# Two-level block matmul on one core: a new order of the steps in a group, and five sums on GpSimd in place of six

## The chip, the cores and the metric

One core of one Trainium2 chip runs the kernel. The metric is the device time of one execution in microseconds; of the kernel before there are three timed runs and one profiled execution. The engines are called as in the profile: PE is TensorE (matmul), PEld its weight load, DVE is VectorE, ACT is ScalarE, POOL is GpSimd, SP is SyncE, whose queue issues the DMAs.

## The reference

```python
def setup_inputs():
    B, S, D = 8, 2048, 2048
    return {
        "x": np.random.randn(B, S, D).astype(np.float32),
        "w": np.random.randn(D, D).astype(np.float32),
    }

def reference(x, w):
    cs = np.cumsum(x, axis=1)
    diff = cs - np.concatenate([np.zeros((cs.shape[0], 1, cs.shape[2]), dtype=np.float32), cs[:, :-1, :]], axis=1)
    return np.matmul(diff, w).astype(np.float32)
```

The differences of a running sum are the numbers themselves, so the output is x times w: 16384 rows by 2048, with 2048 in the contraction.

## The kernel before

The 16384 rows are 128 tiles of 128 rows. Four tiles are multiplied plainly at the start, while w comes in; then tiles are taken in groups of four. From row tile 12 on there are 29 groups, and each runs the same list of named steps (class Group, L988). The four tiles of a group are called g, h, k and l. The weights stay in SBUF as fp16 blocks, and each x tile is scaled row by row into fp16, so that the product can be made from block sums with fewer multiplications (Strassen's scheme in Winograd's form), on two levels.

The outer level makes the sums S1 to S4 of x blocks (128x1024, DVE, L1188 to L1193) and seven products P1 to P7 of a group. Six of these (all but P6) are split once more in the same way. The names of the inner steps, for a product Pn:

- Pn.s1 to Pn.s4: four sums of x quarters, 128x512 fp16, both inputs in SBUF, one instruction each. `total` (L559) puts it on DVE (L563) or, if its name stands in ON_POOL (L557), on POOL (L561).
- Pn.fp4 and the like: a fill, one DVE instruction (128x2048 fp16, L958) that makes a difference of two weight blocks in the tile `flow`, which the quarter Pn.p4 then reads. Both its inputs are in SBUF too. There are eight fills in a group.
- Pn.p1 to Pn.p7: the quarters, four matmuls each (L592). P6 takes eight such pieces (L573).
- merges (m1, a5g, a7k and so on, L1062), copies (cg, c5, cv) and snapshots from one PSUM bank to another or to a tile c: DVE and ACT.
- keep.C.. (ACT), add.C.. (DVE, L603 and L1128), last.C.. (ACT, L600): they bring a piece of the result out of PSUM into a tile c. A DVE step of these reads one input from PSUM. put.C.. (SP) stores it.
- load, weigh0, weigh1, scale, recip, unit, narrow0, narrow1, turn0, turn1 of g, h, k, l: they bring in the x tile of a later group, find a row's size on ACT (L125), turn it into a factor on POOL (scale, unit: L142, L161) and DVE (recip: L156), narrow it to fp16 on ACT (L172) and transpose it by DMA (turn, L185).

A program-wide list, ORDER (L1271), holds all 215 steps of a group in the order in which they are issued. "+1" behind a name means that the step is run for the group after the current one, "+2" for the one after that, "-1" for the one before. `after` (L86) keeps each engine's instructions in that order, so ORDER sets six in-order queues, one for each engine and one for the DMAs. Between engines only data sets the time: an instruction waits for the semaphores of what it reads and of the last readers of the buffer it writes, and then runs as soon as its own queue is free. Small sums live in four scratch quarters (`scratch`, L984): a sum takes the quarter that an earlier product's step has let go, and so waits for that step.

Tiles as the profile names them: x is a transposed x tile, `inner` holds the scratch quarters and some weights, b is a PSUM bank, c a result piece, `flow` the fill, F the loaded x, `of` a row's numbers.

Of the kernel before, what the change touches and what calls it, by code (L numbers as in the profile page):

```python
# [10 lines left out]
def kernel(  # L11
# [540 lines left out]
    def less(dst, p, q):  # L552
        if len(dst.shape) == 4 or len(p.shape) == 4 or len(q.shape) == 4:
            dst, p, q = in_twos(dst), in_twos(p), in_twos(q)
        after("dve", lambda: nc.vector.tensor_tensor(dst, p, q, SUB))

    ON_POOL = "P3.s1 P3.s4 P4.s1 P4.s3 P4.s4 P5.s4".split()  # L557

    def total(dst, p, q, op, pool=False):  # L559
        if pool:  # L560
            after("pool", lambda: nc.gpsimd.tensor_tensor(dst.all, p.all, q.all, op))  # L561
        else:
            after("dve", lambda: nc.vector.tensor_tensor(dst.all, p.all, q.all, op))  # L563
# [479 lines left out]

# [227 lines left out]
    ORDER = """  # L1271
    S1.h+0 S2.h+0 last.C12h1-1 put.C21h1-1 put.C12h1-1 last.C11g1+0 S4.h+0 keep.C22g0+0
    P3.p2+0 P6h.3+0 P5.s1+0 keep.C12g0+0 weigh0.g+1 add.C12g0.z+0 P6h.0+0 P6h.2+0
    P6h.1+0 weigh1.g+1 add.C11h0.q+0 S3.g+0 P5.s3+0 keep.C12g1+0 P7.p1+0 P4.p1+0
    put.C11g1+0 P7.fp5+0 P3.s1+0 put.C11h0+0 S3.h+0 scale.g+1 recip.g+1 P7.s1+0 P7.c1+0
    P3.s3+0 P7.s2+0 put.C11h1+0 P7.a1+0 narrow0.g+1 P7.s3+0 P7.p5+0 P7.s4+0 P7.p6+0
    P7.p2+0 P7.fp7+0 keep.C12h1+0 P5.s2+0 P7.c5+0 P5.p5+0 keep.C21g0+0 P7.c6+0
    add.C22g0.x+0 P7.a5g+0 narrow1.g+1 P4.s1+0 P7.a5h+0 P5.s4+0 P5.ct+0 P7.a6+0 load.h+1
    P7.p7+0 P4.p2+0 add.C21g0.x+0 P4.s2+0 P5.p6+0 turn0.g+1 put.C21g0+0 P7.c7+0 P7.p3+0
    P3.s2+0 weigh0.h+1 P3.p1+0 P5.m1+0 P5.p3+0 weigh1.h+1 P7.a7h+0 put.C22g0+0  # L1280
    add.C12g0.q+0 P5.fp4+0 P5.p7+0 last.C12g0+0 P3.s4+0 turn1.g+1 P3.p6+0 P4.p6+0
    keep.C22g1+0 P5.m2+0 P5.p4+0 scale.h+1 unit.l+0 add.C22g1.x+0 recip.h+1
    add.C12g1.q+0 keep.C12h0+0 P3.p7+0 P3.p3+0 P7.a7k+0 narrow0.h+1 keep.C22h0+0
    put.C12g0+0 keep.C22h1+0 narrow1.h+1 P7.fp4+0 add.C12h1.q+0 add.C12h0.q+0
    add.C12h1.z+0 add.C22h1.x+0 P4.s3+0 unit.g+1 P7.p4+0 keep.C21h1+0 P3.p4+0 P4.p5+0
    P4.s4+0 add.C12h0.z+0 P3.p5+0 put.C22g1+0 keep.C21g1+0 P4.fp4+0 add.C12g1.z+0
    add.C22h0.x+0 add.C12g1.e+0 load.k+1 P4.p3+0 last.C12h0+0 weigh0.k+1 turn0.h+1
    P2.p1+1 P1.p1+1 weigh1.k+1 last.C12g1+0 turn1.h+1 P1.cg+1 add.C21g1.x+0 P1.s1+1
    scale.k+1 recip.k+1 put.C22h0+0 narrow0.k+1 put.C22h1+0 P4.p4+0 P1.s2+1 P1.p5+1
    add.C21g1.q+0 P1.s4+1 P2.s1+1 add.C21h1.e+0 P1.ct+1 put.C12h0+0 P2.s2+1 narrow1.k+1  # L1290
    P1.p6+1 put.C12g1+0 keep.C11g0+1 P1.m1+1 P4.p7+0 add.C21h1.q+0 P1.p2+1 P1.s3+1
    P1.p3+1 load.l+1 P1.p7+1 unit.h+1 unit.k+1 P1.fp4+1 last.C21g1+0 keep.C21h0+0
    P2.s4+1 turn0.k+1 add.C21h0.x+0 P1.m2+1 keep.C11g1+1 P2.p6+1 add.C11g1.q+1 P2.cv+1
    weigh0.l+1 keep.C11h1+1 P2.s3+1 P2.p2+1 P2.p5+1 weigh1.l+1 P1.p4+1 add.C11g0.v+1
    add.C11h1.e+1 turn1.k+1 last.C21h1+0 P2.p7+1 scale.l+1 put.C21h0+0 recip.l+1
    add.C12h1.e+0 S1.g+1 P2.p3+1 P5.p1+1 narrow0.l+1 S2.g+1 P2.fp4+1 P6g.0+1 P6g.1+1
    add.C11h1.q+1 narrow1.l+1 P2.p4+1 add.C11g1.e+1 P5.cg+1 P5.p2+1 put.C21g1+0
    put.C11g0+1 S4.g+1 P3.fp2+1 turn0.l+1 keep.C11h0+1 turn1.l+1 load.g+2 last.C11h1+1
    P6g.3+1 P6g.2+1
    """  # L1300
# [81 lines left out]
```

## Time and profile before

| what | before |
|---|---|
| three timed runs | 1456.04, 1457.63, 1458.39 us (median 1457.63) |
| the profiled execution | 1461.91 us, of which its instructions span 1459.8 us |
| mean granted clock of PE | 0.999 |
| busy: PE, DVE | 1428.9 us (98%), 1398.8 us (96%) |
| busy: ACT, POOL | 1159.6 us (79%), 356.7 us (24%) |
| large sums on POOL (L561) | 174, six in each of 29 groups |
| moved by DMA | 351.65 MB, mean 241 GB/s |

A row of the timeline gives the start in microseconds from the span's start, the duration, engine, line, operation, tiles and shape, and in brackets the idle time before it with what ended it. Rows of one engine whose starts lie closer together than their durations are pipelined: the next instruction starts before the last one's end is recorded. What an instruction costs its engine is then the distance between starts, not the duration. The windows view gives the busy time of each engine in a stretch, with the number of its instructions in brackets. The table of waits gives, for each engine and line, what ended its idle time: the sum in microseconds, how often, and the longest.

### The profile page before, as it was taken

To read this page: it belongs to the slowest core of one execution; us is meant where nothing else is said; L and a number is where in the kernel's file an instruction comes from. 1 tells how busy PE (TensorE), PEld (TensorE's weight loads), DVE (VectorE), ACT (ScalarE), POOL (GpSimd) and SP (SyncE) were. 2 spreads that over 40 slices of the span, in tenths; PEclk is the share of its full clock that TensorE was granted. 3 is DMA by queue.
4 is the path that set the end of the run, shared out by engine and by line. 5 is a ranking of instruction groups with operands and counts; after the bars stand their busy time and mean duration, and the time that the engine had idled before them with its cause. 6 is when DMAs were issued, how large, how long until landed. Compare 5 with 4: busy or idle time off the path is not lost. (4 is left out here: it accounts for less than half of the span.)

```text
span 1459.8 us, 21125 instructions
## 1 busy us (share of the span) xinstructions
PE 1428.9 (98%) x6567; PEld 634.9 (43%) x6567; DVE 1398.8 (96%) x2354; ACT 1159.6 (79%) x1782; POOL 356.7 (24%) x422
## 2 busy tenths in 40 slices
PE   8999999999999999999999999999999999999997
PEld 3444444444444444444444444444444444444443
DVE  7998879999999999999999999999999999999998
ACT  5887568888878888888888888888888888878882
POOL 0101022122322122322223332223321223321221
PEclk9999999999999999999999999999999999999999
DMA  9999858989889999998998899998889988889982
GB/s 361 364 238 299 214 159 224 251 230 237 243 234 232 260 222 245 237 244 228 257 233 246 233 239 237 251 220 251 239 240 238 245 229 257 235 238 238 246 236 104
DMA packets 377761, 351.65 MB, mean 241 GB/s; under 512 B 274800, under 2 KB 274800, under 8 KB 377520
## 3 DMA queue, kind: packets, MB, share of 16 engines
q1 hardware_dynamic: 377088, 348.47, 87.9%
q0 software_dynamic: 560, 1.84, 0.4%
q8 instruction: 51, 0.84, 0.2%
q14 instruction: 62, 0.51, 0.1%
HBM read 150.99 MB, written 134.22 MB: 195 GB/s over the span
## 5 line engine op out<-in xcount | busy, mean ns | idle before, releaser
L592 PE MATMUL b<-W,x 128*128 128x512 f16 x2116 | 519.5, 379 | 5.7 <-DVE x L563 4.1
L592 PEld LDWEIGHTS <-x 128*128 128x128 f16 x2936 | 284.7, 98 | 366.9 <-DVE x L563 17.0
L1128 DVE TENSOR_TENSOR c<-b,c 128x512 f32<-128x512 f32 x504 | 333.5, 680 | 1.8 <-PE b L592 1.7
L172 ACT ACTIVATE F<-F,of 128x1024 f16<-128x1024 f32 x246 | 282.9, 1150 | 32.0 <-DVE of L156 30.4
L125 ACT ACTIVATE waste<-F 128x1024 uint8<-128x1024 f32 x246 | 259.9, 1057 | 56.9 <-DMA F<-in_x_dram 53.8
L592 PEld LDWEIGHTS <-inner 128*128 128x128 f16 x1984 | 190.7, 98 | 248.9 <-DVE inner L563 26.9
L592 PE MATMUL b<-W,inner 128*128 128x512 f16 x1168 | 286.5, 379 | 3.7 <-DVE b L1062 2.3
L573 PE MATMUL b<-W,x 128*128 128x512 f16 x1248 | 285.4, 379 | 1.5 <-DVE x L563 1.3
L603 DVE SCALAR_TENSOR_TENSOR c<-b,of,c 128x512 f32<-128x512 f32 x286 | 210.3, 743 | 12.8 <-PE b L592 5.8
L563 DVE TENSOR_TENSOR x<-x,x 128x1024 f16<-128x1024 f16 (+1 forms) x358 | 211.7, 598 | 10.2 <-DMA x<-F 6.7
L592 PE MATMUL b<-flow,x 128*128 128x512 f16 x812 | 208.3, 379 | 4.8 <-DVE flow L958 3.7
L600 ACT ACTIVATE c<-b,of 128x512 f32<-128x512 f32 x268 | 178.4, 682 | 38.1 <-PE b L592 13.7
L142 POOL TENSOR_SCALAR of<-of 128x1 f32<-128x1 f32 x112 | 80.7, 721 | 474.2 <-ACT waste L125 409.4
L1062 DVE TENSOR_TENSOR b<-b,c 128x512 f32<-128x512 f32 x284 | 188.4, 691 | 1.9 <-ACT c L1087 1.0
L1117 ACT COPY c<-b 128x512 f32<-128x512 f32 x224 | 128.6, 580 | 74.1 <-DVE c L603 46.1
L573 PEld LDWEIGHTS <-x 128*128 128x128 f16 x1248 | 121.6, 98 | 150.0 <-DVE x L563 9.2
L958 DVE TENSOR_TENSOR flow<-W 128x2048 f16<-128x2048 f16 x142 | 179.0, 1260 | 0.0
L600 ACT ACTIVATE c<-c,of 128x512 f32<-128x512 f32 x224 | 154.8, 714 | 14.0 <-DVE c L1128 13.9
L592 PE MATMUL b<-inner 128*128 128x512 f16 x472 | 121.1, 379 | 0.0
L561 POOL TENSOR_TENSOR inner<-x 128x512 f16<-128x512 f16 x29 | 35.8, 1234 | 269.0 <-PE b L592 259.1
L561 POOL TENSOR_TENSOR x<-x,x 128x512 f16<-128x512 f16 x58 | 89.7, 1547 | 21.4 <-PE b L592 21.4
L1087 ACT COPY c<-b 128x512 f32<-128x512 f32 x112 | 66.0, 589 | 24.5 <-PE b L592 10.6
(78 smaller groups left out, 983.9 us busy)
## 6 DMA issues: line engine op xcount, KB each, us to landing
F<-in_x_dram SPq DMA_DIRECT2D x246, 512.0 KB, 5.9
out_dram<-c SPq DMA_DIRECT2D x492, 256.0 KB, 3.2
W<-in_w_dram SPq DMA_DIRECT2D x32, 512.0 KB, 10.1
...
```

The costliest lines, as they stand in the source:

```text
L125: lambda: nc.scalar.activation(waste, where[t][i], ABS, scale=1.0 / ROW, accum_out=sums_of[t][:, i : i + 1],),
L172: lambda: nc.scalar.activation(narrowed(t)[:, ds(i * NH, NH)], where[t][i], COPY, scale=s),
L561: after("pool", lambda: nc.gpsimd.tensor_tensor(dst.all, p.all, q.all, op))
L563: after("dve", lambda: nc.vector.tensor_tensor(dst.all, p.all, q.all, op))
L573: said = nc.tensor.matmul(to[n], a[k], b[k][:, n, :], start=(first and k == 0), stop=(k == KH - 1), skip_group_check=True,)
L592: said = nc.tensor.matmul(to, a[k], b[k], start=(first and k == 0), stop=(k == 3), skip_group_check=True)
L600: after("act", lambda: nc.scalar.activation(c, p, COPY, scale=u))
L603: after("dve", lambda: nc.vector.scalar_tensor_tensor(c, p, u, c, MUL, ADD))
L958: after("dve", lambda: nc.vector.tensor_tensor(in_twos(flow), x, y, op))
L1062: after("dve", lambda: nc.vector.tensor_tensor(t, p, s, ADD))
L1117: after("act", lambda: nc.scalar.copy(to, p))
L1128: after("dve", lambda: nc.vector.tensor_tensor(to, p, to, ADD))
```

## The change

ON_POOL names five sums where there were six: P1.s4, P2.s3, P4.s2, P4.s4 and P5.s4. P3.s1, P3.s4, P4.s1 and P4.s3 go from POOL to DVE, and P1.s4, P2.s3 and P4.s2 from DVE to POOL. ORDER is a new list of the same 215 steps, and its round begins at another point (so some steps that stood as "+0" at its front now stand as "+1" at its end, and weigh0.g, weigh1.g and scale.g as "+2"). Two smaller tables follow from it: in which slots the first group's plain P7 is run (PLAINLY), and which step the first group's one-off weight difference stands before (add.C12h1.e in place of add.C12g1.e). No instruction's shape changes, and the arithmetic is the same.

Cut to its core, with one piece of the list before and after:

```diff
-    ON_POOL = "P3.s1 P3.s4 P4.s1 P4.s3 P4.s4 P5.s4".split()
+    ON_POOL = "P1.s4 P2.s3 P4.s2 P4.s4 P5.s4".split()
...
-    P1.p6+1 put.C12g1+0 keep.C11g0+1 P1.m1+1 P4.p7+0 add.C21h1.q+0 P1.p2+1 P1.s3+1
-    P1.p3+1 load.l+1 P1.p7+1 unit.h+1 unit.k+1 P1.fp4+1 last.C21g1+0 keep.C21h0+0
+    add.C21h1.e+0 P1.ct+1 P1.s4+1 P1.p6+1 unit.k+1 P1.m1+1 P4.p4+0 P4.p7+0 narrow1.k+1
+    add.C21g1.x+0 P2.s1+1 keep.C11g0+1 last.C12h1+0 add.C21h1.q+0 P2.s2+1 P2.cv+1
+    P1.fp4+1 P1.p3+1 keep.C11g1+1 keep.C21h0+0 P1.p7+1 P2.s4+1 weigh0.l+1 turn1.k+1
...
-        "P7.p5": ["P7g.1"],
+        "P7.p5": ["P7g.0", "P7g.1"],
...
-"add.C12g1.e": lambda: less(in_7.t12, in_7.t12, in_7.t11)
+"add.C12h1.e": lambda: less(in_7.t12, in_7.t12, in_7.t11)
```

What stands on POOL in a group, before (two places apart, from the same round of the list). Each row is line, operation, output and inputs, shape; x_63 to x_70 are the eight halves of the four transposed x tiles (x_63 and x_64 of g, x_65 and x_66 of h, x_67 and x_68 of k, x_69 and x_70 of l). The two long runs of sums here are P4.s1, P5.s4, P3.s4, and then P4.s3 and P4.s4; P3.s1 comes last:

```order
L561 TENSOR_TENSOR x_67<-x_70 128x512
L561 TENSOR_TENSOR inner<-x_67,inner 128x512
L561 TENSOR_TENSOR inner<-x_64,inner 128x512
L142 TENSOR_SCALAR of<-of 128x1
L161 TENSOR_SCALAR of<-of,uw 128x1
L561 TENSOR_TENSOR x_70<-x_68,x_70 128x512
L161 TENSOR_SCALAR of<-of,uw 128x1
L561 TENSOR_TENSOR x_69<-x_68,x_67 128x512
L142 TENSOR_SCALAR of<-of 128x1
L161 TENSOR_SCALAR of<-of,uw 128x1 x2
L142 TENSOR_SCALAR of<-of 128x1
L561 TENSOR_TENSOR inner<-x_66 128x512
```

And after, from P1.s4 (the first sum) over P2.s3 and P5.s4 to P4.s2 and P4.s4:

```order
L561 TENSOR_TENSOR inner<-x_63,inner 128x512
L161 TENSOR_SCALAR of<-of,uw 128x1
L561 TENSOR_TENSOR inner<-x_64,x_66 128x512
L142 TENSOR_SCALAR of<-of 128x1 x2
L161 TENSOR_SCALAR of<-of,uw 128x1
L561 TENSOR_TENSOR inner<-x_67,inner 128x512
L142 TENSOR_SCALAR of<-of 128x1
L161 TENSOR_SCALAR of<-of,uw 128x1
L561 TENSOR_TENSOR x_67<-x_67,x_68 128x512
L561 TENSOR_TENSOR x_69<-x_68,x_67 128x512
```

Of the sums only P5.s4 and P4.s4 are on POOL in both; the small instructions between them (scale and unit) are the same in number.

On DVE, around the fill P1.fp4 (the row that reads S_775), before:

```order
L1062 TENSOR_TENSOR b_788<-b_785,c_763 128x512
L1128 TENSOR_TENSOR c_755<-b_787,c_755 128x512
L563 TENSOR_TENSOR inner<-x_63,x_65 128x512
L958 TENSOR_TENSOR flow<-W,S_775 128x2048
L563 TENSOR_TENSOR inner<-x_64,inner 128x512
L603 SCALAR_TENSOR_TENSOR c_751<-b_789,of,c_751 128x512
L1062 TENSOR_TENSOR b_791<-b_785,c_763 128x512
L1128 TENSOR_TENSOR c_771<-b_784,c_771 128x512
L563 TENSOR_TENSOR inner<-x_64,x_66 128x512
```

These are P1.m1, add.C21h1.q, P1.s3, the fill, P2.s4, add.C21h0.x, P1.m2, add.C11g1.q and P2.s3. And after:

```order
L1128 TENSOR_TENSOR c_747<-b_791,c_747 128x512
L563 TENSOR_TENSOR inner<-x_66 128x512
L1128 TENSOR_TENSOR c_767<-b_784,c_767 128x512
L563 TENSOR_TENSOR inner<-inner,x_64 128x512
L958 TENSOR_TENSOR flow<-W,S_775 128x2048
L563 TENSOR_TENSOR inner<-x_64,inner 128x512
L1062 TENSOR_TENSOR b_785<-b_790,c_755 128x512
L1128 TENSOR_TENSOR c_763<-b_789,c_763 128x512
L603 SCALAR_TENSOR_TENSOR c_759<-b_788,of,c_759 128x512
```

These are add.C21g1.x, P2.s1, add.C21h1.q, P2.s2, the fill, P2.s4, P1.m2, add.C11g1.q and add.C21h0.x. P2.s2 and P1.s3 have changed places in front of the fill, and P2.s3 has left DVE for POOL.

More of the change, by code (lines that the diff above doesn't have):

```diff
@@ L1271 @@
     ORDER = """
[L1272 to L1289, printed above, removed]
@@ L1296 @@
[L1296 to L1299, printed above, removed]
+    keep.C12g1+0 S3.h+0 recip.g+1 P7.s1+0 load.h+1 P4.p1+0 P5.s2+0 P7.s2+0 P7.p5+0
+    P7.c1+0 P7.a1+0 narrow0.g+1 P7.s3+0 P7.s4+0 P7.p6+0 P7.fp7+0 P7.c5+0 P7.c6+0 P7.p2+0
+    P3.s1+0 P5.p5+0 add.C22g0.x+0 narrow1.g+1 keep.C12h1+0 P7.a5g+0 P7.a5h+0 P7.p7+0
@@ new lines @@
+    P5.s4+0 P4.p2+0 P5.p6+0 P7.a6+0 put.C22g0+0 keep.C21g0+0 add.C21g0.x+0 P5.ct+0
+    put.C21g0+0 P7.c7+0 P7.p3+0 P3.s3+0 P3.s2+0 weigh0.h+1 P5.m1+0 P3.p1+0 P3.s4+0
+    weigh1.h+1 P5.fp4+0 P5.p7+0 add.C12g0.q+0 keep.C12h0+0 turn0.g+1 P5.m2+0 P5.p3+0
+    P3.p6+0 P5.p4+0 P7.a7h+0 P7.a7k+0 last.C12g0+0 scale.h+1 recip.h+1 add.C12g1.q+0
+    keep.C22g1+0 P3.p3+0 P3.p7+0 keep.C22h0+0 P7.fp4+0 narrow0.h+1 narrow1.h+1 turn1.g+1
+    add.C12g1.z+0 add.C12h1.q+0 put.C12g0+0 P3.p4+0 load.k+1 add.C12h0.q+0 P7.p4+0
@@ new lines @@
+    P4.s1+0 keep.C22h1+0 unit.h+1 add.C12h0.z+0 add.C22h1.x+0 P3.p5+0 add.C12h1.z+0
+    P1.p1+1 last.C12h0+0 keep.C21h1+0 add.C12g1.e+0 weigh0.k+1 P4.p5+0 turn0.h+1
+    add.C22g1.x+0 add.C22h0.x+0 P4.s2+0 P1.cg+1 weigh1.k+1 P4.p6+0 turn1.h+1 put.C22h1+0
+    add.C12h1.e+0 P4.s3+0 P4.s4+0 last.C12g1+0 put.C22h0+0 P1.s1+1 scale.k+1 put.C12h0+0
+    unit.g+1 P2.p1+1 P1.p2+1 put.C22g1+0 put.C12g1+0 recip.k+1 P4.p3+0 load.l+1
+    narrow0.k+1 keep.C21g1+0 P1.s3+1 P1.s2+1 P4.fp4+0 P1.p5+1 add.C21g1.q+0
@@ new lines @@
+    add.C21h1.e+0 P1.ct+1 P1.s4+1 P1.p6+1 unit.k+1 P1.m1+1 P4.p4+0 P4.p7+0 narrow1.k+1
+    add.C21g1.x+0 P2.s1+1 keep.C11g0+1 last.C12h1+0 add.C21h1.q+0 P2.s2+1 P2.cv+1
+    P1.fp4+1 P1.p3+1 keep.C11g1+1 keep.C21h0+0 P1.p7+1 P2.s4+1 weigh0.l+1 turn1.k+1
+    P2.p2+1 weigh1.l+1 P1.m2+1 keep.C11h1+1 turn0.k+1 P2.p6+1 add.C11g1.q+1 P2.s3+1
+    P2.p5+1 add.C21h0.x+0 scale.l+1 P1.p4+1 add.C11h1.e+1 recip.l+1 S1.g+1 P2.p7+1
+    last.C21h1+0 put.C21h0+0 P2.p3+1 narrow0.l+1 S2.g+1 P2.fp4+1 add.C11h1.q+1
@@ new lines @@
+    add.C11g1.e+1 S4.g+1 P5.p1+1 put.C12h1+0 P6g.0+1 narrow1.l+1 P6g.2+1 last.C11h1+1
+    P5.cg+1 P2.p4+1 add.C11g0.v+1 P5.p2+1 P6g.3+1 P6g.1+1 last.C11g1+1 keep.C22g0+1
+    put.C21h1+0 P3.fp2+1 turn0.l+1 keep.C11h0+1 P3.p2+1 turn1.l+1 S1.h+1 load.g+2 S2.h+1
+    P5.s1+1 P6h.1+1 put.C11h1+1 last.C21g1+0 keep.C12g0+1 weigh0.g+2 P6h.2+1 weigh1.g+2
+    put.C21g1+0 add.C11h0.q+1 scale.g+2 P5.s3+1 S4.h+1 P6h.3+1 unit.l+1 P6h.0+1 S3.g+1
+    P7.p1+1 put.C11h0+1 put.C11g0+1 put.C11g1+1 P7.fp5+1 add.C12g0.z+1
```

13 lines of the change are left out of this document (5 added, 8 removed).

## The prediction

> **What bounds the kernel now.** I read the page first, to see which engines are full.
>
> ```profile
> span 1459.8 us, 21125 instructions
> PE 1428.9 (98%) x6567; PEld 634.9 (43%) x6567; DVE 1398.8 (96%) x2354; ACT 1159.6 (79%) x1782; POOL 356.7 (24%) x422
> ```
>
> PE and DVE are both nearly full. Which of them sets the pace is a question for the stretch in which the groups repeat, so I took windows next: first the 27 full groups between two instructions that occur once in each, then one undisturbed group and one disturbed.
>
> ```profile
> core 0: us, PE busy (x) PEld busy (x) DVE busy (x) ACT busy (x) POOL busy (x), PEclk, DMA share, GB/s
> 223.80:1411.29 1187.49, 1175.47 (x5402) 522.46 (x5400) 1162.26 (x1999) 983.56 (x1540) 321.39 (x378) 1.00 0.90 239
> 708.63:751.94 43.31, 43.31 (x202) 19.42 (x200) 42.84 (x76) 36.50 (x59) 12.10 (x14) 1.00 0.91 242
> 971.53:1016.55 45.02, 43.93 (x202) 19.12 (x200) 43.71 (x76) 36.30 (x58) 11.11 (x14) 1.00 0.91 233
> ```
>
> A group takes 1187.49 / 27 = 43.98 us on average, 43.31 undisturbed. PE has 200 matmuls in it (5400 weight loads in 27 groups). What one costs PE is read from a run of eight, from its start to the next run's:
>
> ```profile
> 749.56 1.89 PE L592 MATMUL b<-W,x 128*128 128x512 f16 x8
> 751.29 1.89 PE L592 MATMUL b<-W,inner 128*128 128x512 f16 x8
> ```
>
> (751.29 - 749.56) / 8 = 0.216, so PE's own work is 200 x 0.216 = 43.2 us, and only 0.78 us of a group is to be won on PE. DVE's own work comes from the distances between starts:
>
> ```profile
> 708.63 1.22 DVE L958 TENSOR_TENSOR flow<-W,S 128x2048 f16<-128x2048 f16 x1
> 709.77 0.42 DVE L563 TENSOR_TENSOR inner<-x,inner 128x512 f16<-128x512 f16 x1
> 710.10 0.74 DVE L603 SCALAR_TENSOR_TENSOR c<-b,of,c 128x512 f32<-128x512 f32 x1
> 710.76 0.69 DVE L1062 TENSOR_TENSOR b<-b,c 128x512 f32<-128x512 f32 x1
> 711.36 0.68 DVE L1128 TENSOR_TENSOR c<-b,c 128x512 f32<-128x512 f32 x1
> 711.96 0.42 DVE L563 TENSOR_TENSOR inner<-x,x 128x512 f16<-128x512 f16 x1
> 713.55 0.16 DVE L156 RECIPROCAL of<-of 128x1 f32<-128x1 f32 x1
> 713.63 0.67 DVE L1128 TENSOR_TENSOR c<-b,c 128x512 f32<-128x512 f32 x1
> 188.46 0.69 DVE L563 TENSOR_TENSOR x<-x,x 128x1024 f16<-128x1024 f16 x1
> 189.07 1.22 DVE L555 TENSOR_TENSOR F<-W 128x2048 f16<-128x2048 f16 x1
> ```
>
> A fill costs 1.14, a small sum 0.33, an L603 add 0.66, an L1062 or L1128 step 0.60, a large sum (1024 wide) 0.61, a reciprocal 0.08. A group's DVE list has 8 fills, 18 small sums, 8 L603, 28 of L1062 and L1128, 8 large sums and 4 reciprocals: 9.12 + 5.94 + 5.28 + 16.80 + 4.88 + 0.32 = 42.34 us. That is close under PE's 43.2, and DVE has more to wait for. Who waits for whom in the same 27 groups:
>
> ```profile
> DVE of L156 <- POOL of L142: 10.1, 45, 0.8
> DVE x L563 <- DMA x<-F: 6.7, 10, 1.3
> DVE b L1062 <- ACT c L1087: 1.0, 2, 0.6
> DVE c L603 <- PE b L592: 0.6, 1, 0.6
> DVE b L1062 <- PE b L592: 0.2, 1, 0.2
> PE b L592 <- DVE x L563: 4.1, 6, 0.9
> PE b L592 <- DVE flow L958: 3.5, 6, 0.7
> ```
>
> PE waits for DVE; of the 1187.49 - 1162.26 = 25.2 us that DVE is idle, it waits for PE in this list 0.8 us only, and most of the rest for POOL's scale and for transposes. So DVE with its waits is the pace, and time added to DVE is not covered by anything.
>
> **The change part by part.** Sums moved: four go from POOL to DVE, three from DVE to POOL. DVE has one more, 0.33 a group: 42.67.
>
> The POOL sums: POOL is 24% busy, so their length costs nothing by itself. What matters is what they do to DVE. Two places of the trace show it:
>
> ```profile
> 189.46 1.84 POOL L561 TENSOR_TENSOR inner<-x 128x512 f16<-128x512 f16 x1 [22.22 <-PE b L592]
> 190.20 1.38 DVE L563 TENSOR_TENSOR inner<-x 128x512 f16<-128x512 f16 x1
> 1002.19 0.81 PE L592 MATMUL b<-flow,x 128*128 128x512 f16 x3
> 1003.09 1.16 POOL L561 TENSOR_TENSOR x<-x,x 128x512 f16<-128x512 f16 x1 [0.49 <-PE b L592]
> 1003.22 2.10 DVE L958 TENSOR_TENSOR flow<-W 128x2048 f16<-128x2048 f16 x1
> 1005.38 0.81 PE L592 MATMUL b<-flow,x 128*128 128x512 f16 x3 [0.65 <-DVE flow L958]
> ```
>
> At 1003 POOL's sum (P4.s4) starts 0.13 us ahead of the fill P7.fp4, and the fill ends 0.9 later than the 1.22 of an ordinary one; PE then stands. At 189 POOL's sum is asked for in the middle of the long DVE instruction of 189.07, whose inputs also both lie in SBUF. It waits for that to end at 190.29 and takes its 1.0 until 191.30, and the next DVE sum, issued at 190.20, takes 1.38 in place of 0.42. So a POOL sum and a DVE instruction with two SBUF inputs exclude each other, and a POOL sum that is waiting goes ahead of the next of them. Beside DVE steps that read PSUM, POOL sums cost DVE nothing: L1128 keeps its 0.60.
>
> Where do the five fall? Each starts when its data is there, wherever the list puts it. P4.s2 is released by DVE's P4.s1, with seven PSUM steps (over 4 us) behind it: P4.s2 and P4.s4 fit. P5.s4 follows P5.p5 on PE, beside PSUM merges. P1.s4 is released by P1.s2 with the fill P4.fp4 right behind: POOL waits 1.1, and then finds PSUM steps; its reader P1.p3 comes later still. That leaves P2.s3. It needs the scratch quarter that P1.p7 reads. In the new list PE runs P4.p7, P1.p3, P1.p7 in a row, four matmuls each, so P1.p7 ends 2 x 4 x 0.216 = 1.73 after P4.p7. On DVE, add.C21h1.q waits for P4.p7, and behind it come P2.s2 and the fill P1.fp4: the fill starts 0.60 + 0.33 = 0.93 after P4.p7 at the earliest. P1.p7 thus ends 0.80 or less behind the fill's start. POOL starts 0.09 behind a PE end (1003.09 against 1002.19 + 0.81). So POOL asks within 0.9 of the fill's start, and P2.s4, with two SBUF inputs, is issued 1.14 after it. Whatever else moves, this meets the picture of 189.46: P2.s4 takes 1.38, +0.96, in each group. If DVE is later by a microsecond, POOL comes first and the fill itself pays the same. In the order before, P2.s3 stands on DVE, and nothing of the kind is there.
>
> One place speaks otherwise. A small POOL instruction at the start of the span sits 1.36 us through two DVE instructions with two SBUF inputs, and these keep their 3.68 / 6 = 0.61:
>
> ```profile
> 89.76 1.36 POOL L161 TENSOR_SCALAR of<-of,uw 128x1 f32<-128x1 f32 x1 [9.69 <-DVE of L147]
> 89.78 3.68 DVE L550 TENSOR_TENSOR W<-W 128x1024 f16<-128x1024 f16 x6
> ```
>
> By that row P2.s4 would pay nothing. I take 0.96, since the row of 189.46 shows a whole POOL sum and this one a single element. The Trainium skill's page "SBUF — State Buffer" ("Who interferes with whom") says that a VectorE instruction with two SBUF inputs contends with a GpSimd instruction that reads SBUF, and that whichever issues first holds the pair for its whole length. By it POOL, which asks before P2.s4 is issued, goes first: +0.96, not 0.
>
> Gone: P4.s4's clash with P7.fp4, since P4.s4 now waits for P4.s2. The waits list has PE standing six times for a fill; 6 x (2.10 - 1.22) / 27 = -0.20. S1.g's wait for its transposes is part of the 6.7 us; P2.s4's delay lies in front of S1.g and covers it: -0.10 (from 0 to -0.25, which is all of 6.7 / 27). DVE's waits for PE and ACT vanish when DVE is late: 0.6 + 0.2 + 1.0, and of the some 6 us of idle that the list leaves below its bounds about half: 5 / 27 = -0.19. The waits for POOL's scale (10.1 / 27 = 0.37) hang on the same chains of load, weigh, scale in both orders, with steps on both sides of each moved by half a microsecond: 0, from -0.37 to +0.3. The order of the puts and turns on SP, the units on POOL and the PLAINLY slots touch one group or have slack: nothing, within 1 us in all.
>
> Sum: 0.33 + 0.96 - 0.20 - 0.10 - 0.19 = +0.80 us a group; over 28 groups +22.4. As a cross-check, 42.67 + 0.96 = 43.63 of DVE work alone is already above PE's 43.2. The profiled execution took 1461.91 us, its span 1459.8; the median of the runs is 1457.63, 4.3 lower, and I set the change on that: 1480.0.
>
> **The rivals.** (1) *DVE keeps the pair.* POOL's P2.s3 would wait through P2.s4 too, and then run beside PSUM steps at no cost. For it speaks the small instruction at 89.76, against it the sum at 189.46, the only one of its kind.
> Then DVE has 42.67, the clash at P7.fp4 is gone, and the disturbed groups come down towards the clean 43.31: (43.98 - 43.5) x 28 = -13, about 1444, with the extra 0.33 taken out of the 0.47 that DVE idles in the clean group. It decides when P2.s4 shows 0.42 and not 1.38. Faster: 0.25.
>
> (2) *Nothing in sum.* The changes on POOL do not bite (its sums start when data is there, so that a place further ahead in the list moves none of them), P2.s3 costs nothing, and the one more sum eats what the clash gave back: 0.33 - 0.20 - 0.10 = 0.03 a group, 1 us, 1458. Same: 0.13.
>
> **How the numbers follow.** Forecast (P2.s4 pays): 0.62. Its own range: with all the 6.7 and 10.1 us of waits gone, 0.33 + 0.96 - 0.20 - 0.25 - 0.37 - 0.19 = +0.28, 8 us; with nothing absorbed and the scale waits longer, 0.33 + 0.96 - 0.20 + 0.3 = +1.39, of which I leave out the far end: 1465 to 1490. Rival (1) spans 1438 to 1453. For 8 in 10 I take 1446 to 1490, which leaves out the lower half of rival (1) and the far end of the forecast. A measurement of this kernel can tell about 0.2%, 3 us, from no change; faster 0.25, same 0.13, slower 0.62.
>
> **What would show it.** Right: the sum behind P1.fp4 (L563, inner<-x,inner) near 1.38 in nearly every group, with an L561 of about 1.5 to 2 us that starts inside that fill; a group near 44.8 us; PE idle for DVE b L1062 and c L1128 behind it; no fill of 2.1 at P7.fp4. Wrong: P2.s4 at 0.42, or a DVE with more idle time than before.

## The result, and the profile after

The changed kernel takes 1502.21 us (median of 4 runs, 1499.42 to 1504.11) beside 1458.01 for the kernel before (4 runs, 1456.04 to 1460.93). The ratio is 1.0299, with a 95% interval of 1.0286 to 1.0312: slower by 44 us. The direction was as forecast, the size twice what was forecast, and 12 us outside the range. One run of a later experiment (e7) took 5361.78 us, three and a half times as long as its other runs, and is not counted in that kernel's median.

From the page after, and from the windows view of 27 full groups between the same two markers as before (the L958 instruction that reads S):

```profile
span 1501.4 us, 21121 instructions
PE 1446.7 (96%) x6561; PEld 635.8 (42%) x6567; DVE 1425.8 (95%) x2383; ACT 1161.7 (77%) x1782; POOL 323.3 (22%) x393
```

```profile
224.42:1454.04 1229.62, 1196.17 (x5401) 523.67 (x5400) 1190.10 (x2026) 986.20 (x1540) 285.49 (x351) 1.00 0.89 231
```

A group takes 1229.62 / 27 = 45.54 us, 1.56 more than before. DVE's busy time went from 1162.26 to 1190.10, by 27.8 us; its idle time went from 25.2 to 39.5, by 14.3. So two thirds of the loss are DVE's own instructions, and one third is waiting that wasn't there before. The forecast had the first part to within 2 us (0.33 + 0.96 - 0.20 is 1.09 a group, 29.4 in 27), and had the second with the other sign; more idle time on DVE than before is one of the two signs of being wrong that it names.

The first part, in the timeline of one group, DVE and then POOL:

```profile
725.73 0.42 DVE L563 TENSOR_TENSOR inner<-inner,x 128x512 f16<-128x512 f16 x1
726.06 1.22 DVE L958 TENSOR_TENSOR flow<-W,S 128x2048 f16<-128x2048 f16 x1
727.19 1.38 DVE L563 TENSOR_TENSOR inner<-x,inner 128x512 f16<-128x512 f16 x1
728.50 0.69 DVE L1062 TENSOR_TENSOR b<-b,c 128x512 f32<-128x512 f32 x1
```

```profile
726.32 1.98 POOL L561 TENSOR_TENSOR inner<-x,x 128x512 f16<-128x512 f16 x1 [2.78 <-PE b L592]
```

This is the forecast picture: POOL asks for P2.s3 0.26 us into the fill P1.fp4, has it for 1.98 us, and P2.s4 behind the fill shows 1.38 where it needs 0.42. It is so in 28 of 29 groups, and nowhere else does POOL cost DVE anything: P1.s4 waits through a fill too (2.02 us on POOL), but DVE steps that read PSUM follow that fill, and they keep their 0.68 and 0.69. The fill P7.fp4, which lost 0.9 in some groups before, shows 1.22 in all.

The second part, in the table of waits for the same 27 groups:

```profile
DVE b L1062 <- ACT c L1087: 11.8, 18, 1.2
DVE of L156 <- POOL of L142: 10.6, 44, 1.2
DVE x L563 <- DMA x<-F: 7.0, 10, 1.2
DVE c L1128 <- ACT c L1117: 3.2, 7, 1.1
```

The first row was 1.0 us before, the last wasn't there, and the two between stand as they were (10.1 and 6.7). The first is one place: the merge P7.a1, which waits for the copy P7.c1 on ACT. What P7.c1 waits for, in one group (DMA issues, ACT, PE and DVE):

```profile
out_dram<-c SPq DMA_DIRECT2D x1, 256.0 KB, 5.9
```

```profile
742.96 0.57 ACT L1117 COPY c<-b 128x512 f32<-128x512 f32 x1
744.78 0.58 ACT L1087 COPY c<-b 128x512 f32<-128x512 f32 x1 [1.25 <-DMA out_dram<-c]
```

```profile
742.74 1.89 PE L592 MATMUL b<-W,x 128*128 128x512 f16 x8
```

```profile
745.40 0.70 DVE L1062 TENSOR_TENSOR b<-b,c 128x512 f32<-128x512 f32 x1 [0.34 <-ACT c L1087]
```

The DMA row is the store put.C21g1 alone, issued at 738.85: it takes 5.9 us to land, where the page has 3.4 as the median of all stores. The first four matmuls of the row at 742.74 are P7.p1, which P7.c1 reads; the bank is there at 743.77. But the c tile that P7.c1 writes is the one that put.C21g1 is still reading, until 744.7. So ACT stands 1 us longer than PE makes it, and DVE waits 0.34 behind it. In the order before, P7.c1 took the tile of another store, put.C12h1, and DVE waited some 1 us in 27 groups. That store stood behind the loads of g too, and took longer still to land, here 6.8 us (SP, then DMA issues):

```profile
717.66 1.01 SPq L113 DMA_DIRECT2D F<-in_x_dram  x2
718.72 1.81 SPq L614 DMA_DIRECT2D out_dram<-c  x3
```

```profile
out_dram<-c SPq DMA_DIRECT2D x1, 256.0 KB, 6.8
```

It was issued sooner, though: counted from the start of the fill P2.fp4, put.C12h1 was issued at 3.69 us and landed at 10.6 in the order before, and put.C21g1 is issued at 6.14 and lands at 12.1 now (medians). ACT's waits for a store's landing in front of its L1087 copies, of which P7.c1 is one, in 27 groups before and after:

```profile
ACT c L1087 <- DMA out_dram<-c: 8.2, 16, 1.4
ACT c L1087 <- DMA out_dram<-c: 32.0, 25, 1.9
```

### The profile page after: what moved, and what is told of

Same layout as the page of the kernel before. It is cut to its first block, busy times and chain, and to the rows that moved or that the text cites. A ratio compares the mean times of both kernels' runs of the same rounds, so it can differ in the third digit from the quotient of the medians.

```text
span 1501.4 us, 21121 instructions
## 1 busy us (share of the span) xinstructions
PE 1446.7 (96%) x6561; PEld 635.8 (42%) x6567; DVE 1425.8 (95%) x2383; ACT 1161.7 (77%) x1782; POOL 323.3 (22%) x393
## 5 line engine op out<-in xcount | busy, mean ns | idle before, releaser
L592 PE MATMUL b<-W,x 128*128 128x512 f16 x2116 | 508.5, 379 | 5.5 <-DVE c L603 2.0
L592 PEld LDWEIGHTS <-inner 128*128 128x128 f16 x1984 | 191.5, 97 | 277.3 <-issue 49.1
L592 PE MATMUL b<-W,inner 128*128 128x512 f16 x1168 | 290.8, 378 | 13.9 <-DVE b L1062 4.4
L573 PE MATMUL b<-W,x 128*128 128x512 f16 x1248 | 285.6, 379 | 2.2 <-DVE x L563 2.0
L592 PE MATMUL b<-flow,x 128*128 128x512 f16 x812 | 208.3, 379 | 10.7 <-DVE b L1062 10.6
L563 DVE TENSOR_TENSOR x<-x,x 128x1024 f16<-128x1024 f16 x358 | 209.1, 598 | 9.3 <-DMA x<-F 7.0
L600 ACT ACTIVATE c<-c,of 128x512 f32<-128x512 f32 x224 | 161.1, 719 | 70.0 <-DVE c L1128 70.0
L142 POOL TENSOR_SCALAR of<-of 128x1 f32<-128x1 f32 x112 | 56.3, 503 | 586.4 <-ACT waste L125 517.9
L958 DVE TENSOR_TENSOR flow<-W 128x2048 f16<-128x2048 f16 x142 | 173.5, 1222 | 0.0
L561 POOL TENSOR_TENSOR inner<-x,inner 128x512 f16<-128x512 f16 x58 | 91.0, 1569 | 168.1 <-PE b L592 159.2
L592 PE MATMUL b<-inner 128*128 128x512 f16 x472 | 116.3, 379 | 4.4 <-DVE c L1128 4.2
L561 POOL TENSOR_TENSOR x<-x,x 128x512 f16<-128x512 f16 x58 | 67.2, 1158 | 177.9 <-DMA F<-in_x_dram 117.0
L1087 ACT COPY c<-b 128x512 f32<-128x512 f32 x112 | 63.4, 585 | 44.1 <-DMA out_dram<-c 32.0
```

Of the source, the lines that this page charges most:

```text
L573: said = nc.tensor.matmul(to[n], a[k], b[k][:, n, :], start=(first and k == 0), stop=(k == KH - 1), skip_group_check=True,)
L592: said = nc.tensor.matmul(to, a[k], b[k], start=(first and k == 0), stop=(k == 3), skip_group_check=True)
L600: after("act", lambda: nc.scalar.activation(c, p, COPY, scale=u))
L958: after("dve", lambda: nc.vector.tensor_tensor(in_twos(flow), x, y, op))
```

## The experiments

Sixteen kernels were run, each in five rounds beside the kernel before. Its medians in these four sittings were 1458.2, 1458.4, 1459.4 and 1459.0, so that medians can be compared across them to within about 1 us. The columns of this table: the median, the length of the 27 groups in the profiled execution, DVE's busy time in them, and the difference, its idle time.

| kernel | us | 27 groups | DVE busy | DVE idle |
|---|---|---|---|---|
| before | 1458.0 | 1187.5 | 1162.3 | 25.2 |
| after | 1502.2 | 1229.6 | 1190.1 | 39.5 |
| e1: P2.s3 on DVE | 1489.5 | 1216.7 | 1173.8 | 42.9 |
| e2: one PSUM step ahead of P2.s4 | 1491.5 | 1218.5 | 1174.5 | 43.9 |
| e3: two PSUM steps | 1488.5 | 1214.8 | 1165.6 | 49.1 |
| e4: put.C21g1 far ahead | 1500.4 | 1226.2 | 1189.2 | 37.1 |
| e6: last.C21g1 two places ahead | 1508.9 | 1233.2 | 1190.0 | 43.2 |
| e7: e6, and P2.s4 ahead of the fill | 1515.0 | 1242.4 | 1192.2 | 50.3 |
| e8: new ORDER, old POOL sums | 1526.6 | 1253.3 | 1196.7 | 56.6 |
| e9: old ORDER, new POOL sums | 1507.7 | 1233.4 | 1208.0 | 25.4 |
| l1: before, light stores | 1448.6 | 1175.6 | 1161.8 | 13.8 |
| l2: after, light stores | 1476.5 | 1203.7 | 1186.6 | 17.1 |
| l3: e3, light stores | 1450.9 | 1179.5 | 1163.0 | 16.5 |
| e10: e3 and e4 | 1496.6 | 1224.3 | 1165.5 | 58.8 |
| e11: put.C21g1 left out | 1486.5 | 1212.9 | 1187.5 | 25.4 |
| e12: last and put of C21g1 in gaps | 1487.3 | 1214.6 | 1187.7 | 26.9 |
| e13: e3, weigh1.l behind keep.C11h1 | 1482.4 | 1209.9 | 1166.2 | 43.7 |
| e14: e12 and e13 | 1471.2 | 1199.8 | 1165.3 | 34.5 |

### Take the clash away: e1, e2, e3

The first theory was that P2.s4 is on the path in every group; its rival, that the list itself holds the group. e1 takes P2.s3 off POOL:

```diff
-    ON_POOL = "P1.s4 P2.s3 P4.s2 P4.s4 P5.s4".split()
+    ON_POOL = "P1.s4 P4.s2 P4.s4 P5.s4".split()
```

> The kernel after with P2.s3 taken back from POOL to DVE (four sums on POOL). Theory A (DVE is the pace, and the 0.96 us that P2.s4 loses to POOL's P2.s3 is on the path in each of 28 groups): P2.s4 falls from 1.38 to 0.42, DVE gets one more sum of 0.33; 28 x (0.33 - 0.96) = -18, from 1502 to 1484 us. Theory B (the new list is slow by itself: something other than DVE's instructions, above all the copy P7.c1 that waits for the transfer put.C21g1, holds the group at 45.5 us, and time saved on DVE becomes more waiting there): 1497 us or more, and DVE's idle time in front of P7.a1 grows from 11 us to 20 or more.

e2 puts one step that reads PSUM between the fill and P2.s4 (first diff), e3 two, P1.m2 and add.C21h0.x (second diff, the list without its line breaks):

```diff
-    P1.fp4+1 P1.p3+1 keep.C11g1+1 keep.C21h0+0 P1.p7+1 P2.s4+1 weigh0.l+1 turn1.k+1
-    P2.p2+1 weigh1.l+1 P1.m2+1 keep.C11h1+1 turn0.k+1 P2.p6+1 add.C11g1.q+1 P2.s3+1
+    P1.fp4+1 P1.p3+1 keep.C11g1+1 keep.C21h0+0 P1.p7+1 weigh0.l+1 turn1.k+1 P2.p2+1
+    weigh1.l+1 P1.m2+1 P2.s4+1 keep.C11h1+1 turn0.k+1 P2.p6+1 add.C11g1.q+1 P2.s3+1
```

> The kernel after with P2.s4 moved behind P1.m2, so that one DVE step that reads PSUM (0.60) stands between the fill P1.fp4 and P2.s4; POOL keeps P2.s3. Theory A (POOL takes about 1.0 us as soon as the fill ends, PSUM steps run beside it, and only a DVE instruction with two SBUF inputs has to wait for the rest): P1.m2 stays at 0.69, P2.s4 loses 0.96 - 0.60 = 0.36 and shows 0.75 to 0.85; 28 x -0.60 = -17, 1485 us. A rival on the mechanism (whatever DVE runs next behind the fill pays): P1.m2 shows 1.65 and the time stays at 1502. Theory B: 1497 or more.

```diff
-    P1.p7+1 P2.s4+1 weigh0.l+1 turn1.k+1 P2.p2+1 weigh1.l+1 P1.m2+1 keep.C11h1+1
+    P1.p7+1 weigh0.l+1 turn1.k+1 P2.p2+1 weigh1.l+1 P1.m2+1 add.C21h0.x+0 P2.s4+1 keep.C11h1+1
...
-    P2.p5+1 add.C21h0.x+0 scale.l+1
+    P2.p5+1 scale.l+1
```

> The kernel after with P2.s4 moved behind P1.m2 and add.C21h0.x, so that two DVE steps that read PSUM stand between the fill P1.fp4 and P2.s4; POOL keeps P2.s3. Theory A: POOL is through before P2.s4 is issued; P2.s4 0.42, 28 x -0.96 = -27, 1475 us, less what DVE may wait for the keep of C21h0, which the move brings nearer (up to 5 us). Theory B: 1497 or more.

The mechanism came out as expected. DVE in e2, from the fill on, and then in e3:

```profile
721.56 1.22 DVE L958 TENSOR_TENSOR flow<-W,S 128x2048 f16<-128x2048 f16 x1
722.69 0.69 DVE L1062 TENSOR_TENSOR b<-b,c 128x512 f32<-128x512 f32 x1
723.29 0.78 DVE L563 TENSOR_TENSOR inner<-x,inner 128x512 f16<-128x512 f16 x1
```

```profile
717.80 1.22 DVE L958 TENSOR_TENSOR flow<-W,S 128x2048 f16<-128x2048 f16 x1
718.94 0.69 DVE L1062 TENSOR_TENSOR b<-b,c 128x512 f32<-128x512 f32 x1
719.54 0.74 DVE L603 SCALAR_TENSOR_TENSOR c<-b,of,c 128x512 f32<-128x512 f32 x1
720.20 0.41 DVE L563 TENSOR_TENSOR inner<-x,inner 128x512 f16<-128x512 f16 x1
```

P2.s4 takes 1.38, 0.78 and 0.41 with none, one and two PSUM steps ahead of it: the first step, 0.60 from start to start, covers 0.60 of POOL's sum, the second the rest, and neither costs anything itself, since both only stand at another place. The time didn't follow in full. DVE's busy time in 27 groups fell by 16.3, 15.6 and 24.5 us, the groups by 12.9, 11.2 and 14.9: what DVE saved came back in part as idle time. In e3 most of it sits at one place, add.C11h1.e (12.7 us, from 2.7), which waits for ACT's keep.C11h1:

```profile
DVE c L1128 <- ACT c L1117: 12.8, 18, 1.9
DVE of L156 <- POOL of L142: 11.3, 40, 1.5
DVE b L1062 <- ACT c L1087: 10.2, 16, 1.2
DVE x L563 <- DMA x<-F: 7.0, 10, 1.1
```

So neither theory held as stated: the clash is on the path, but something close behind it takes back part of what its removal saves, 3.4, 4.4 and 9.6 us in 27 groups.

### Two tries at the store, and two crossed kernels: e4, e6, e7, e8, e9

e4 moves last.C21g1 behind last.C21h1 and put.C21g1 behind put.C21h0, 34 and 38 places ahead in the list (its expectation says some 20). P7.c1 then takes the tile of put.C11h1:

```diff
+    last.C21h1+0 last.C21g1+0 put.C21h0+0 put.C21g1+0 P2.p3+1 narrow0.l+1
...
-    P6h.1+1 put.C11h1+1 last.C21g1+0 keep.C12g0+1 weigh0.g+2 P6h.2+1 weigh1.g+2 put.C21g1+0
+    P6h.1+1 put.C11h1+1 keep.C12g0+1 weigh0.g+2 P6h.2+1 weigh1.g+2
```

> The kernel after with last.C21g1 moved on ACT to stand behind last.C21h1 and put.C21g1 on SP to stand behind put.C21h0, some 20 places ahead of where the new list has them; the c tile that the copy P7.c1 takes is then the one of put.C11h1, issued over 2 us sooner than put.C21g1. P2.s4 keeps its 1.38. Theory A: DVE's 11.1 us of idle in front of P7.a1 in 27 groups go and nothing takes their place: 1502 - 11.5 = 1490 to 1492 us. Theory C (the transfers themselves are the limit, DMA being 0.89 busy): the wait moves to another copy or to the transposes, and the time stays within 3 us of 1502.

The wait at P7.a1 went, as expected, and the time fell by under 2 us only. The wait came up in front of S1.h, which reads the transposes of l:

```profile
DVE x L563 <- DMA x<-F: 21.3, 28, 1.8
DVE c L1128 <- ACT c L1117: 1.6, 4, 0.5
```

SP's queue shows why: in e4 (first fence) four stores stand together in front of the two transposes of l, and these follow without a gap; in the kernel after (second fence) there are three, and SP is free for 0.9 us ahead of the transposes.

```profile
728.30 2.58 SPq L614 DMA_DIRECT2D out_dram<-c  x4
730.98 2.81 SPq L185 DMA_TRANSPOSE x<-F  x2
```

```profile
730.46 1.30 SPq L614 DMA_DIRECT2D out_dram<-c  x3
732.69 2.62 SPq L185 DMA_TRANSPOSE x<-F  x2
```

Taken over the groups and from the fill P2.fp4, the second transpose is issued 0.5 us later (1.87 for 1.36) and lands 0.9 later. The next expectation lays this to narrow0.l on ACT; the trace does not bear that out (narrow0.l starts 1.20 us ahead of P2.fp4 in both): the delay begins on SP.

e6 leaves SP's order alone and brings last.C21g1 two places ahead on ACT, behind last.C11g1. e7 adds P2.s4 ahead of the fill:

```diff
-    P1.fp4+1 P1.p3+1 keep.C11g1+1 keep.C21h0+0 P1.p7+1 P2.s4+1 weigh0.l+1 turn1.k+1
+    P1.p3+1 P2.s4+1 P1.fp4+1 keep.C11g1+1 keep.C21h0+0 P1.p7+1 weigh0.l+1 turn1.k+1
...
-    P5.cg+1 P2.p4+1 add.C11g0.v+1 P5.p2+1 P6g.3+1 P6g.1+1 last.C11g1+1 keep.C22g0+1
+    P5.cg+1 P2.p4+1 add.C11g0.v+1 P5.p2+1 P6g.3+1 P6g.1+1 last.C11g1+1 last.C21g1+0
```

> The kernel after with only last.C21g1 moved, on ACT from behind keep.C11h0 to behind last.C11g1 (two places, into a gap in which ACT waits for PE), so that put.C21g1 is issued some 1.2 us sooner and no step of the tiles' own chain (narrow, turn, load) is put behind it, as last.C21g1 was put ahead of narrow0.l in the run with put.C21g1 20 places ahead. Theory D (two waits beside DVE are in turn what is latest: the copy P7.c1 for put.C21g1, and the transposes of l for S1.h; the run before moved time from one to the other because its edit delayed narrow0.l by one ACT step of 0.6): the 11 us in front of P7.a1 go, S1.h stays near 6 us; 1490 to 1494. Theory C (the transfers themselves bound the group, so that a wait removed comes up elsewhere whatever the place): within 3 us of 1502.

> The kernel after with last.C21g1 as in the run before it and P2.s4 (with P1.p3 on PE's queue) ahead of the fill P1.fp4, so that POOL's P2.s3 falls behind the fill beside PSUM steps. DVE's own work falls by the 0.96 of P2.s4, 26 us in 27 groups, and the wait in front of P7.a1 goes. Theory D: more than either alone, 1502 - 27 - 11 = 1464 if nothing else comes up, and up to 1475 with add.C11h1.e and S1.h waiting more, as they did where P2.s4 alone was moved. Theory C: 1485 or more, as where P2.s4 alone was moved (1488).

Both expectations missed. In e6 the store was issued 1.8 us sooner (4.35 us after P2.fp4 for 6.14, medians) and landed 0.5 us later (12.61 for 12.09). Still behind the loads of g, it took 8.2 us from issue to landing (median, for 6.0); one of them:

```profile
out_dram<-c SPq DMA_DIRECT2D x1, 256.0 KB, 8.2
```

```profile
DVE b L1062 <- ACT c L1087: 17.7, 23, 1.3
```

In e7 the clash did not go, it moved. P2.s4 ahead of the fill makes the fill 0.33 later, POOL's P2.s3 asks before the fill starts, and the fill pays. First DVE, then POOL:

```profile
729.83 0.42 DVE L563 TENSOR_TENSOR inner<-x,inner 128x512 f16<-128x512 f16 x1
730.17 2.18 DVE L958 TENSOR_TENSOR flow<-W,S 128x2048 f16<-128x2048 f16 x1
```

```profile
729.90 1.37 POOL L561 TENSOR_TENSOR inner<-x,x 128x512 f16<-128x512 f16 x1 [2.77 <-PE b L592]
```

e8 and e9 cross the two halves of the change: the new ORDER with the old ON_POOL, and the old ORDER with the new one.

```diff
-    ON_POOL = "P1.s4 P2.s3 P4.s2 P4.s4 P5.s4".split()
+    ON_POOL = "P3.s1 P3.s4 P4.s1 P4.s3 P4.s4 P5.s4".split()
```

> The new ORDER with the old set of six sums on POOL (P3.s1, P3.s4, P4.s1, P4.s3, P4.s4, P5.s4). P2.s3 is on DVE, and DVE has one sum fewer than in the kernel after. By DVE's instructions alone: 28 x (0.96 + 0.33) = 36 us less, 1466. Theory D (part of what DVE saves comes back as waiting for P7.c1, keep.C11h1 and the transposes, as in the three runs that removed the clash): 1475 to 1485, above the old order's 1458 with the same pool sums.

> The old ORDER with the new five sums on POOL. In the old list too the fill P1.fp4 follows the DVE step that releases P1.p7 (P1.s3), and P2.s4 follows the fill; P1.p7 takes four matmuls, 0.86, so that POOL asks for P2.s3 before the fill's 1.14 are over. So P2.s4 should show 1.38 here as well: 28 x (0.33 + 0.96) = 36, less some 8 us of DVE waits covered, 1480 to 1494. If the clash belongs to the new order, P2.s4 stays at 0.42 and the time is 1458 to 1468.

Both crossings are slower than the kernel after, e8 by 24 us and e9 by 5, and both have clashes at other places than those named. In e9 P2.s4 keeps its 0.41 in every group, against the expectation; instead P2.s1 takes 1.06, P4.s1 0.62 and P7.fp4 1.95, and DVE's idle time stays as before (25.4). P7.fp4 and the sum P4.s4 that does it:

```profile
804.12 1.95 DVE L958 TENSOR_TENSOR flow<-W 128x2048 f16<-128x2048 f16 x1
```

```profile
803.83 1.15 POOL L561 TENSOR_TENSOR x<-x,x 128x512 f16<-128x512 f16 x1 [1.56 <-issue]
```

In e8 P5.fp4 takes 1.85 and P1.s1 1.05, and DVE waits 11.3 us for PE in front of add.C11g1.q, which no run here takes apart. Order and set belong together: with the other list's set, POOL's sums meet two-SBUF-input instructions in nearly every group. With its own set the old list has this in 6 of 27 groups (P7.fp4), and the new one in all 27 (P2.s4, through P2.s3).

### Make the transfers lighter: l1, l2, l3, and e10

The light kernels store a quarter of each result piece, and change nothing else:

```diff
-        after("sp", lambda: nc.sync.dma_start(out2[ds(t * P, P), ds(at * NB, NB)], c))
+        after("sp", lambda: nc.sync.dma_start(out2[ds(t * P, P), ds(at * NB, NB // 4)], c[:, : NB // 4]))
```

> The kernel before with each store of a group's result cut to a quarter: 128 of a piece's 512 columns are written, the other three quarters are left out (64 KB in place of 256 KB; all loads, transposes and sums stay). Theory C' (the stores, loads and transposes of a group queue up behind one another, and DVE's and ACT's waits for them are what is left besides DVE's own instructions): the waits in front of S1.h and S1.g, 7 us in 27 groups, go, and those for the scale partly; 1440 to 1452. If transfers do not matter: 1458.

> The kernel after with the same cut of the stores to a quarter. Theory C': the 12 us in front of P7.a1 (put.C21g1's landing) go, and the 7 us in front of S1.h and S1.g and the 3 of add.C11h1.e with them, while P2.s4 keeps its 1.38: 1502 - 22 = 1478 to 1484. If the waits come from the engines' order and not from the transfers: 1495 or more.

> The kernel after with P2.s4 behind two PSUM steps (no clash with POOL's P2.s3) and the same cut of the stores. With full stores this edit gave 14 us of the 27 that P2.s4 lost. Theory C': the other half was eaten by waits for transfers, so with light stores it gives 24 to 27 us against the run with light stores and the clash: 1453 to 1460. If what ate it are the engines' own orders (ACT's above all), it gives some 14 again: 1465 to 1470.

> The kernel after with full stores and two edits together: P2.s4 behind two PSUM steps (alone 1488) and last.C21g1 and put.C21g1 20 places ahead (alone 1500). Alone, the first was held by P7.c1's wait for put.C21g1 in 16 of 25 groups and the second by the transposes of l. If the two waits are the only ones besides DVE's work, and the saved DVE time lies on the path from recip.k to recip.l that the second one leaves, it gives 1500 - 24 = 1473 to 1478. If the transfers as a whole hold the group (theory C), it stays at 1485 or more.

The three light runs came out at the expected places. The windows of 27 groups, l1, l2 and l3 in turn:

```profile
223.60:1399.15 1175.55, 1170.26 (x5401) 524.29 (x5400) 1161.77 (x2000) 982.17 (x1540) 319.87 (x378) 1.00 0.69 169
```

```profile
223.67:1427.38 1203.71, 1185.24 (x5401) 525.84 (x5400) 1186.63 (x2027) 989.26 (x1540) 285.60 (x351) 1.00 0.66 165
```

```profile
223.86:1403.33 1179.47, 1174.56 (x5401) 527.03 (x5400) 1163.00 (x2027) 986.10 (x1540) 280.98 (x351) 1.00 0.68 169
```

With light stores the two kernels differ by 27.9 us and not by 44 (1476.5 and 1448.6): in 27 groups 24.9 us of DVE's busy time, and only 3.3 of its idle time (17.1 and 13.8). There the clash costs its full price: l2 less l3 is 25.5 us, where the same edit gave 14 with full stores. And without clash and without full stores the new order is 2.4 us behind the old (1450.9 and 1448.6). So some 16 of the 44 us go when the stores carry a quarter of the bytes, 11 of them idle time of DVE. The wait at P7.a1 is gone in l2, though put.C21g1 still stands behind the same loads of g: it lands 3.1 us after its issue (median; 6.0 in the kernel after). e10 shows that it is not cured by e3 and e4 together: S1.h waits 27.5 us in place of 19.3, since DVE, faster, reaches it sooner.

### One store, or the queue as a whole: e11 to e14

e11 leaves out one of the 16 stores of a group and moves nothing. e12 keeps it, and puts last.C21g1 into a gap of ACT (behind keep.C21h0, where ACT stands for load.l) and put.C21g1 ahead of put.C21h0. The first diff is e11's, the second e12's; the two steps' old places go as in e4:

```diff
-            self.step(f"put.{c}", lambda: put(self.at.pop(c), self.row(c), n))
+            self.step(f"put.{c}", lambda: free.append(self.at.pop(c)) if c == "C21g1" else put(self.at.pop(c), self.row(c), n))
```

```diff
-    P1.fp4+1 P1.p3+1 keep.C11g1+1 keep.C21h0+0 P1.p7+1 P2.s4+1 weigh0.l+1 turn1.k+1
+    P1.fp4+1 P1.p3+1 keep.C11g1+1 keep.C21h0+0 last.C21g1+0 P1.p7+1 P2.s4+1 weigh0.l+1
...
-    last.C21h1+0 put.C21h0+0 P2.p3+1 narrow0.l+1
+    last.C21h1+0 put.C21g1+0 put.C21h0+0 P2.p3+1 narrow0.l+1
```

> The kernel after with one of a group's 16 stores left out, put.C21g1 (that piece of the result is not written): the copy P7.c1 then waits for PE alone, and no engine's order changes. Theory E (put.C21g1 stands behind load.g on the queue and lands 12.1 us after the fill P2.fp4, 1 us behind the end of P7.p1; that alone costs DVE the 12 us in front of P7.a1): 1490 us, P7.a1 without idle time, S1.h still near 6. Rival (the queue of transfers as a whole holds the group, and the wait comes up in front of S1.h or recip.g): 1496 or more.

> The kernel after, all stores in, with last.C21g1 put on ACT behind keep.C21h0 (where ACT stands 0.7 us for load.l) and put.C21g1 on SP ahead of put.C21h0 (where few transfers are under way); narrow0.l isn't delayed this time, as it was in the first try, and the store is ahead of load.g, as it was not in the second. P7.c1 gets put.C11h1's tile, which lands at 9.8 us after P2.fp4. Theory E: P7.a1 without idle time, S1.h near 6, 1490. Rival: the 256 KB ahead of the transposes of l make S1.h wait 10 us more; 1498 to 1502.

Both came out below what was expected, 1486.5 and 1487.3, with P2.s4 still at 1.38. In e12 the same store lands 2.8 us after its issue, P7.c1 starts 0.03 us behind P7.p1, and no row is left for ACT's L1087:

```profile
out_dram<-c SPq DMA_DIRECT2D x1, 256.0 KB, 2.8
```

```profile
DVE of L156 <- POOL of L142: 9.9, 38, 1.3
DVE x L563 <- DMA x<-F: 7.6, 9, 1.3
DVE c L1128 <- ACT c L1117: 2.8, 5, 1.0
```

P7.c1 now takes another tile, that of put.C11h1, which stands behind the loads of g as well but lands some 2 us sooner, about 10.0 us after P2.fp4 for 12.1. So it was the late landing of one store, and the queue has room for that store a few microseconds earlier; e11 shows the cause, e12 that nothing has to be left out. At this place that settles it against the rival.

e13 takes e3 and lets keep.C11h1 go ahead of weigh1.l on ACT (weigh1.l waits for load.l's landing); e14 adds e12's two moves to it. The diff is e13's against e3:

```diff
-    P2.p2+1 weigh1.l+1 P1.m2+1 add.C21h0.x+0 P2.s4+1 keep.C11h1+1 turn0.k+1
+    P2.p2+1 P1.m2+1 add.C21h0.x+0 P2.s4+1 keep.C11h1+1 weigh1.l+1 turn0.k+1
```

> The kernel after with P2.s4 behind two PSUM steps (alone 1488, where DVE came to wait 12.7 us for keep.C11h1 in front of add.C11h1.e) and weigh1.l moved on ACT behind keep.C11h1, so that keep.C11h1 no longer stands behind an instruction that waits for load.l. Theory E: those 10 us more go, 1478; if recip.l (which hangs on weigh1.l) waits instead: 1486 to 1490.

> The three edits together on the kernel after: P2.s4 behind two PSUM steps, weigh1.l behind keep.C11h1, last.C21g1 and put.C21g1 in the gap. Theory E (single places, each curable): 1502 - 27 - 11 = 1464 to 1470. Rival (the transfers as a whole, which with light stores gave 1451): 1480 or more.

e13 gave 6 us beyond e3, not 10: add.C11h1.e no longer waits, and recip.l, which hangs on weigh1.l, waits 5.2 us. e14 came to 1471.2, 31 us below the kernel after and 1 us above what was expected of it:

```profile
224.33:1424.13 1199.80, 1182.83 (x5401) 524.12 (x5400) 1165.28 (x2026) 988.02 (x1540) 286.69 (x351) 1.00 0.91 237
```

```profile
DVE of L156 <- POOL of L142: 16.6, 52, 1.0
DVE x L563 <- DMA x<-F: 9.4, 12, 1.3
```

It is 12.3 us behind the kernel before, and its 27 groups likewise (1199.8 and 1187.5): 3.0 more of DVE's busy time and 9.3 more of idle, 6.3 of them at recip.l (8.0 for 1.7) and 3.4 at P1.m1. No version with all its stores whole beats the kernel before.

## Why the prediction was right in direction and wrong in size

Its sum, term by term, in us a group, beside what the 27 groups show (measured from start to start of DVE's instructions, after less before):

| term | forecast | measured |
|---|---|---|
| one more sum on DVE | +0.33 | +0.34 |
| P2.s4 pays for P2.s3 on POOL | +0.96 | +0.97 |
| P4.s4's clash with P7.fp4 gone | -0.20 | -0.18 |
| the rest of DVE's busy time | 0 | -0.10 |
| waits: S1.g -0.10, PE and ACT -0.19, scale 0 | -0.29 | +0.53 |
| sum | +0.80 | +1.56 |

**What held.** DVE with its waits is the pace: with light stores nine tenths of the two kernels' difference are DVE's busy time. P2.s4 at 1.38 behind the fill in nearly every group, P2.s3 at 1.98 on POOL, P4.s2 and P4.s4 free of charge, P7.fp4 at 1.22: all as written. So rival (1), that DVE keeps the pair, is out at this place, and e2 and e3 give the price as a function of what stands between. The rule of the Trainium skill's page "SBUF — State Buffer" ("Who interferes with whom"), that whichever issues first holds the pair, gave the right side: POOL, which asks during the fill, goes ahead of P2.s4 in 28 groups. Rival (2) is out with it.

**What failed.** The step "DVE's waits for PE and ACT vanish when DVE is late", taken at -0.19 a group, together with "the order of the puts and turns on SP, the units on POOL and the PLAINLY slots touch one group or have slack: nothing, within 1 us in all". The order of the puts had no such slack. In the new order P7.c1 gets the tile of put.C21g1, which lands 1.5 us later after P2.fp4 than the store whose tile it got before; P7.c1 waited for a store's landing 3.9 us in 27 groups before (5 groups), and 29.7 us in 26 after (22 groups). That made 11.1 us of new waiting at P7.a1 in 27 groups. Without it the time is 16 us lower (e11) or 15 (e12). The rest of the +0.53 are small places: P1.m1, which now stands right behind add.C21h1.e on DVE (3.4 us in 27 groups), add.C11h1.e (2.7), and some that became shorter: S1.g by 1.1, where 2.7 were forecast. The waits for the scale stand as they were, as forecast (10.8 us at the recips, for 11.0). The miss of 0.82 a group in the waits (+0.53 for -0.29) times 28 is 23 us, and the forecast missed by 22.

The reasoning behind the failed step was that a DVE that is slower everywhere is waited for, and waits less. It holds for waits whose cause does not move with DVE. P7.c1's cause does. In the kernel after, the steps from one DVE instruction to the next one that waits for it stand at fixed distances from the fill P2.fp4 (medians over 24 groups, in us; those up to the store's issue are the same to 0.01 from group to group but for P5.p2's start):

| step | from P2.fp4 |
|---|---|
| add.C11h1.q (DVE) ends | 1.82 |
| last.C11h1, P5.cg (ACT) | 1.85, 2.51 |
| P5.p2 (PE) ends | 4.15 |
| keep.C22g0, keep.C11h0, last.C21g1 (ACT) | 4.24, 4.82, 5.39 |
| put.C21g1 issued, landed | 6.14, 12.09 |
| P7.c1 (ACT) | 12.17 |
| P7.a1 (DVE) | 12.80 |

DVE's own steps from P2.fp4 to P7.a1 take 12.05 (the least of the 24 groups). The chain through ACT, PE, ACT and the store takes 12.80, and both begin at the same DVE instructions: a late DVE moves the two together and gains nothing. The store's landing is the link that varies, from 9.8 to 13.7 us after P2.fp4.

**A second point that the forecast had no term for.** The clash's price and the store's are not simply added. With full stores the removal of the clash gave 14 of its 26 us (e3), after the ACT order around load.l was mended 20 (e13), and with light stores 25.5. What then holds DVE hangs on a landing: that of load.l in front of add.C11h1.e (e3) and recip.l (e13, e14), and that of put.C21g1 in front of P7.a1 (e3, e13). That these few waits are all of it is not shown: from e12 to e14, with put.C21g1 out of the way in both, the removal with e13's move gave 16.

**What stays open.** Why put.C21g1 lands as late as it does no run here settles, nor why it landed later when it was issued 1.8 us sooner (e6). The Trainium skill's page "DMA: Bandwidth & Descriptors" ("Queues, rings and completion order") says that the signal of a transfer's end comes only after all earlier writes of the same DMA engine. The runs agree with it in so far as put.C21g1 lands 6.0 us after its issue behind the 1 MB of loads (median, after) and 2.9 ahead of them (e12). But put.C12h1 stood behind the same loads in the order before and landed in time for P7.c1 in 22 of 27 groups, and in l2 the loads stand ahead of a store that lands in 3.1 us; so the loads alone do not make it late, and that it should land later for being issued sooner doesn't follow from the rule.
